# Sums joined in PSUM, a modulation pass issued earlier, and four triangular solves divided between two engines

## The chip, the core and the metric

The kernel runs on one core of a Trainium2 chip. The core has a matrix engine (TensorE, PE in the profile, with its weight loads shown as PEld), a vector engine (VectorE, DVE), an activation engine (ScalarE, ACT) and a general engine (GpSimd, POOL). SyncE (SP) only issues transfers. Every engine works through its own instructions in a fixed order and waits on semaphores. SBUF is the on-chip memory; PSUM holds the sums of TensorE in eight banks of 128 partitions x 512 f32. The metric is device time in microseconds (us) of one execution. The kernel of before took 1477.43 us, the median of three executions (1477.26 to 1480.0).

## The reference

One layer: an RMS norm with a modulation computed from `c`, one input projection whose columns are split over three groups of heads, an output projection, and a feed-forward block with a squared ReLU. There are 1024 latent tokens and 256 context tokens, and the width is 1024.

```python
def _project(h, lp, rope):
    z = h @ lp['w_in']
    f, aq, ak, av, dqkv, dz, gates = jnp.split(z, SPLITS, axis=-1)
    ...

def _chunk_gdn(q, k, v, g, beta, s0):          # chunks of 64 tokens, 4 heads
    ...
    lmat = jnp.where(strict, jnp.einsum('nbhid,nbhjd->nbhij', kb, kc) * decay, 0.0)
    tmat = lax.linalg.triangular_solve(eye + lmat, jnp.broadcast_to(eye, lmat.shape),
                                       left_side=True, lower=True)
    u = jnp.einsum('nbhij,nbhjd->nbhid', tmat, vb)
    ...
    s_fin, o = lax.scan(step, s0, (qc, kc, u, w, gc, qk))
```

The kernel uses chunks of 32 rows (its CK). The scan runs over them in two directions (d = 0 and 1), and each direction needs the inverse of a unit triangular matrix for every chunk and head. There are 32 latent and 8 context chunks.

## The kernel before

**Numbers.** A matmul operand is split into two parts, hi (rounded to f32r) and lo (the remainder), and a product is three matmuls into one bank: `mm3`, lines 238 to 241 (hi·hi, hi·lo, lo·hi). Single matmuls are issued by `mm` at line 236, transposes by `tp` at line 244, nearly all ACTIVATE instructions by `act` at line 223. In the rows below a line of a helper therefore stands for many callers, and the tile's name tells them apart.

**Stages, in us of the profiled execution.** Up to about 38, the first two modulation vectors are computed. Up to about 125 runs the k and v phase: for pairs of token tiles, `norm_in`, `trans_mod` (transposes, modulation, split into hi and lo) and `proj_N(w_kv, ...)` with `kv_sink`, which stores each tile in DRAM (`kvd`, line 524) after POOL's line 517; the k projection of the scan group, its convolution and the gates belong to the same stretch. From 125 to 205, q is projected in two halves of eight tiles (`proj_N(w_q, ...)`, `q_sink`, `qk_rows`, lines 499 to 517). From 205 to 345 the scan group's v and q are projected and convolved (`conv_proj`, `conv_silu`), and z and the Fourier columns are projected (`dz_f`, which stores z at line 818). Attention follows with the scan beside it (345 to 725), then the output projection (to 831), the second half's h of the feed-forward block (`h2_second`, in 831 to about 905), and the feed-forward products to the end.

**Modulation vectors.** `mod_steps` (line 314) computes one of six vectors from `w_mod`. For each of eight row blocks it loads a slab of 128 x 1024 f32 (512 KB) with an SP transfer (line 321), multiplies it in four matmuls (line 323, shown as L236) that fill four 32-row strips of one bank, and yields. Vectors 0 and 1 are needed first. The late ones are 3, 4, 2 and 5: vector 3 is computed by `mod_pass` ahead of the q projection, and 4, 2 and 5 in the task `modulations` (line 749), over two slab buffers (`msl`).

**Tasks.** `tick()` (line 450) is called inside projections after a few matmuls. It advances the generators in `tasks`, each given as [generator, every so many ticks, so many steps]. From the second half of q on these are `systems` (1, 3), `system1` (1, 1) and `modulations` (2, 1). `systems` first lets 12 steps pass, then runs `grams`: five rounds of 32 small matmuls on TensorE (line 706), two DVE products (line 709) and two stores to DRAM each. It then solves triangular systems: `solve(d, lat, eng)` loads its rows from DRAM and makes 30 elimination steps of two dependent instructions, a product (line 729) into `tmps[d]` and a sum (line 730). DVE solves the two context systems (32 partitions) step by step in turn, then latent direction 0 (128 partitions); POOL solves latent direction 1 from the end of `grams` on. Midway in `dz_f` (n == 3) both generators are run to their end.

**Order.** Instructions go to a scheduler that simulates a timeline and fixes each engine's order at build time. From the second half of q on, TensorE's instructions stay in program order (`pinned`). In the k and v phase they do not.

**Feed-forward block.** It multiplies 2 x 2 blocks of matrices with seven products in place of eight. `h2_second` (line 1539) transposes and modulates the second half of h and forms the sums of blocks that the products need (t1 to t4). The first half's blocks exist only as hi and lo (`HB["11"]`, `HB["21"]`), so a block is subtracted in two instructions, hi and then lo (line 1540). `split` (line 1454) makes the hi and lo of a result, with ACT rounding and the named engine subtracting. Each instruction covers 128 x 512.

Of the kernel before, what the change touches and what calls it, by code (L numbers as in the profile page):

```python
# [194 lines left out]
def body(tc, t, out):  # L195
# [3 lines left out]
    with ctx:  # L199
# [114 lines left out]
        def mod_steps(q, slabs, bank, queue=Y):  # L314
            w = t["w_mod"]
            for k in range(KT):
# [7 lines left out]
                yield  # L324
# [47 lines left out]
        def trans_mod(xs, a, s, hi, lo, banks, c0=0):  # L372
            w = len(xs) * P
            for k in range(KT):
# [6 lines left out]
                (G if k % 2 else V).tensor_tensor(lo[:, k, c0 : c0 + w], hf, f32(hi[:, k, c0 : c0 + w]), op=ALU.subtract)  # L381

# [43 lines left out]
        for b in slab0[4:] + slab1 + xTb:  # L426
            b.free()
# [98 lines left out]
        trb.items = bk[2:5]  # L526
# [6 lines left out]
        for b in xb + slab0[0:4] + hfb + [junkb]:  # L533
            b.free()
# [10 lines left out]
        msl = [buf(D) for _ in range(2)]  # L545
        mslr = Ring([b() for b in msl])
# [148 lines left out]
        done = []  # L695

        def grams():
            for c in list(range(NCL, NCA, 8)) + list(range(0, NCL, 8)):
# [12 lines left out]
                yield  # L711
            done.append(1)
# [3 lines left out]
        def solve(d, lat, eng):  # L716
# [7 lines left out]
            G.memset(Z2.base[pr_, at_ : at_ + S : CK + 1], 1.0)  # L724
# [10 lines left out]
        def systems():  # L735
            for _ in range(3 * GRAM):
                yield
            yield from grams()
            pair = [solve(d, False, V) for d in range(2)]
            while sum(next(x, 1) is None for x in pair):  # L740
                yield
            yield from solve(0, True, V)

        def system1():
            while not done:
                yield
            yield from solve(1, True, G)

        def modulations():
            (v,) = mod_rows(bk[2], 1, rowtmp())  # L750
            V.tensor_tensor(kt2(s2()), v, kt2(col[:, r_b2 : r_b2 + 8]), op=ALU.add)
            yield
            yield from mod_steps(4, mslr, bk[2])
            act(rowtmp(), bk[2][:, 0:256])
            yield
            (v,) = mod_rows(bk[2], 1, rowtmp())
            V.tensor_tensor(kt2(a2()), v, kt2(col[:, r_b2 + 8 : r_b2 + 16]), op=ALU.add)
            V.scalar_tensor_tensor(a2(), a2(), 1.0, col[:, r_n2 : r_n2 + 8], op0=ALU.add, op1=ALU.mult)
            yield
            for q, z in ((2, 0), (5, 1)):  # L760
                yield from mod_steps(q, mslr, bk[2])
                act(mrowb[z](), bk[2][:, 0:256])
                yield
# [1020 lines left out]
```

## Time and profile before

| | |
|---|---|
| three executions, median (lowest to highest) | 1477.43 us (1477.26 to 1480.0) |
| profiled execution, its own time | 1475.22 us |
| profiled execution, span of its trace | 1473.1 us |
| busy in the span: PE, DVE, ACT, POOL | 1391.9, 1026.7, 704.6, 657.2 us |
| mean granted TensorE clock | 0.972 |

The profiled execution is 2.21 us under the median and 2.1 us longer than its span. A row of the view of groups reads: line, engine, operation, output tile <- input tiles, shape, count | busy time and mean duration | idle time of that engine just before these instructions, and what ended it. A row of a timeline begins with start and duration in us. The clock is given as a share of full speed.

### The profile page before, as it was taken

To read this page: it belongs to the slowest core of one execution; us is meant where nothing else is said; L and a number is where in the kernel's file an instruction comes from. 1 tells how busy PE (TensorE), PEld (TensorE's weight loads), DVE (VectorE), ACT (ScalarE), POOL (GpSimd) and SP (SyncE) were. 2 spreads that over 40 slices of the span, in tenths; PEclk is the share of its full clock that TensorE was granted. 3 is DMA by queue.
4 is the path that set the end of the run, shared out by engine and by line. 5 is a ranking of instruction groups with operands and counts; after the bars stand their busy time and mean duration, and the time that the engine had idled before them with its cause. 6 is when DMAs were issued, how large, how long until landed. Compare 5 with 4: busy or idle time off the path is not lost.

```text
span 1473.1 us, 28890 instructions
## 1 busy us (share of the span) xinstructions
PE 1391.9 (94%) x11438; PEld 1118.6 (76%) x11438; DVE 1026.7 (70%) x1747; ACT 704.6 (48%) x1239; POOL 657.2 (45%) x698
## 2 busy tenths in 40 slices
PE   5899888989999999989899789999999999999998
PEld 1787866766777777768799667888888888888886
DVE  0876688775878777786733898755556677676884
ACT  1743312223777777776512645554555443443331
POOL 2764653632446466465433866444343100020782
PEclk8799999989999999999999889999999999999999
DMA  9414374552001010042222214544445898776641
GB/s 327 176 58 141 95 186 122 148 109 79 9 9 25 5 36 10 10 148 72 87 82 105 92 49 143 164 152 156 158 157 185 296 395 271 249 236 210 200 158 57
DMA packets 137302, 197.65 MB, mean 134 GB/s; under 512 B 45021, under 2 KB 80463, under 8 KB 136911
## 3 DMA queue, kind: packets, MB, share of 16 engines
q1 hardware_dynamic: 136464, 195.12, 41.2%
q8 instruction: 89, 1.46, 0.4%
q10 hardware_dynamic: 703, 0.69, 0.2%
q14 instruction: 46, 0.38, 0.1%
HBM read 149.84 MB, written 45.94 MB: 133 GB/s over the span
## 4 chain that ended last, share of the span: by engine, by line
PE 46%; DVE 5%; POOL 2%; issue 1%; DMA 1%; ACT 0%; DVEq 0%; POOLq 0%; ACTq 0%; SPq 0%
PE bk L240 8%; PE bk L241 8%; PE bk L239 8%; PE ba L239 7%; PE ba L240 7%; PE ba L241 7%; DVE fbase L1540 1%; PE bk L236 1%; DVE z1c L1454 1%; DVE z1b L1321 0%; DVE rbase L984 0%; DMA fbase<-la 0%; POOL rbase L1454 0%; PE ba L236 0%; POOL z2c L1714 0%
## 5 line engine op out<-in xcount | busy, mean ns | idle before, releaser
L223 ACT ACTIVATE rbase<-fbase 128x512 fp32r<-128x512 f32 (+3 forms) x255 | 171.9, 686 | 87.6 <-PE bk L240 55.3
L223 ACT ACTIVATE fbase<-bk 128x512 f32<-128x512 f32 (+3 forms) x224 | 124.9, 561 | 150.8 <-PE bk L236 93.8
L236 PE MATMUL bk<-rbase 128*128 128x256 f32 (+1 forms) x960 | 164.5, 307 | 2.1 <-DVE rbase L984 1.1
L236 PEld LDWEIGHTS bk<-rbase 128*128 128x128 f32 (+1 forms) x960 | 127.0, 173 | 30.4 <-DVE rbase L984 1.9
L236 PE MATMUL ba<-rbase 128*65 128x512 f32 (+4 forms) x576 | 137.7, 341 | 6.3 <-DVE rbase L984 4.6
L223 ACT ACTIVATE z1c<-fbase 128x512 fp32r<-128x512 f32 (+1 forms) x120 | 76.7, 654 | 135.3 <-DMA fbase<-w_ff 49.1
L223 ACT ACTIVATE fbase<-fbase 128x512 f32<-128x512 f32 (+4 forms) x148 | 95.8, 660 | 94.5 <-POOL fbase L1606 27.2
L1487 POOL TENSOR_TENSOR fbase<-fbase 128x512 f32<-128x512 f32 x64 | 89.2, 1395 | 110.7 <-DVE z1c L1454 101.5
L1688 POOL TENSOR_TENSOR z2c<-z2c,fbase 128x512 f32<-128x512 f32 x16 | 31.8, 2010 | 203.6 <-ACT z2c L223 128.6
L960 DVE TENSOR_REDUCE fbase<-ba 128x1 f32<-128x512 f32 (+1 forms) x192 | 106.4, 594 | 19.6 <-PE ba L236 18.2
L223 ACT ACTIVATE rbase<-z1d 128x1024 fp32r<-128x1024 f32 x61 | 63.1, 1055 | 101.2 <-PE bk L240 87.3
L1454 DVE TENSOR_TENSOR z1c<-fbase,z1c 128x512 fp32r<-128x512 f32 x112 | 96.3, 866 | 19.2 <-ACT z1c L223 15.8
L1454 DVE TENSOR_TENSOR rbase<-z1d,rbase 128x1024 fp32r<-128x1024 f32 x61 | 85.5, 1416 | 31.8 <-ACT rbase L223 31.7
L984 POOL TENSOR_TENSOR rbase<-fbase,rbase 128x512 fp32r<-128x512 f32 x56 | 72.1, 1288 | 67.2 <-ACT rbase L223 63.1
L239 PE MATMUL bk<-rbase 128*128 128x512 f32 x256 | 99.6, 389 | 0.0
L240 PE MATMUL bk<-rbase 128*128 128x512 f32 x256 | 99.6, 389 | 0.0
L241 PE MATMUL bk<-rbase 128*128 128x512 f32 x256 | 99.6, 389 | 0.0
L984 DVE TENSOR_TENSOR rbase<-fbase,rbase 128x512 fp32r<-128x512 f32 x104 | 81.0, 779 | 24.6 <-ACT rbase L223 23.9
L1454 DVE TENSOR_TENSOR rbase<-fbase,rbase 128x1024 fp32r<-128x1024 f32 (+1 forms) x63 | 79.7, 1285 | 22.6 <-ACT rbase L223 22.5
L236 PEld LDWEIGHTS ba<-rbase 128*65 128x65 f32 (+1 forms) x576 | 75.7, 154 | 23.9 <-DVE rbase L984 5.7
L240 PE MATMUL ba<-rbase 128*128 128x512 f32 x192 | 74.7, 389 | 0.0
L241 PE MATMUL ba<-rbase 128*128 128x512 f32 x192 | 74.7, 389 | 0.0
(346 smaller groups left out, 3842.6 us busy)
## 6 DMA issues: line engine op xcount, KB each, us to landing
fbase<-w_ff SPq DMA_DIRECT2D x70, 512.0 KB
u<-fbase SPq DMA_DIRECT2D x112, 256.0 KB
z1d<-w_ff SPq DMA_DIRECT2D x34, 512.0 KB
z1d<-u SPq DMA_DIRECT2D x33, 512.0 KB
fbase<-w_mod SPq DMA_DIRECT2D x32, 512.0 KB
fbase<-u SPq DMA_DIRECT2D x23, 512.0 KB
z2a<-w_mod SPq DMA_DIRECT2D x16, 512.0 KB
fbase<-w_in SPq DMA_DIRECT2D x16, 512.0 KB
```

The source lines that it names most:

```text
L223: return SC.activation(o, i, f, **k)
L236: pe(T.matmul(o, l, r, start=start, stop=stop))
L239: pe(T.matmul(o, lh, rh, start=start, stop=False))
L240: pe(T.matmul(o, lh, rl, start=False, stop=False))
L241: pe(T.matmul(o, ll, rh, start=False, stop=stop))
L960: V.tensor_reduce(st4[:, z : z + 1], b, AX.X, ALU.max)
L984: (G if k2 in GP and not any(a <= n < b for a, b in NGP) else V).tensor_tensor(hl[:, :, 1], p, f32(hl[:, :, 0]), op=ALU.subtract)
L1454: eng.tensor_tensor(lo, i, f32(hi), op=ALU.subtract)
L1487: G.tensor_tensor(w[nm], w[a], w[b], op=op)
L1540: sub = lambda e, o, i, x: e.tensor_tensor(o, i, x, op=ALU.subtract)
L1688: G.tensor_tensor(c, c, G2[cs_.start // 512], op=ALU.mult)
```

## The change

It has three parts.

**Sums joined in PSUM.** In `h2_second`, where a block is subtracted as hi and then lo, TensorE now multiplies hi and lo by the identity (`idb`, one new copy) into one bank of `tr2`, the ring of the transposes, and DVE subtracts that bank in one instruction. The splits of t3 and all subtractions of POOL in this function go to DVE.

**All late modulation vectors in the k and v phase.** `modulations` now computes vectors 3, 4, 2 and 5 and runs as a task from the start of the k and v phase, over five slab buffers and two slabs to a visit (`many`). `trans_mod` ticks too. Bank `bk[2]` is kept for it, so the transposes use `bk[3]`, `bk[4]` and `bk[1]` and the projection's ring is four banks. What is left of the task is run out after the last k and v tile.

**Solves.** DVE solves direction 0, context and then latent; POOL solves direction 1, context and then latent. Both tasks make three steps at every second tick. The wait ahead of `grams` is 4 steps in place of 12, and each of its rounds yields twice. The latent systems get buffers of their own (`trib`). At n == 3 only the context solves are run to their end.

```diff
@@ mod_steps, trans_mod @@
-        def mod_steps(q, slabs, bank, queue=Y):
+        def mod_steps(q, slabs, bank, queue=Y, many=1):
...
-                yield
+                if k % many == many - 1:
+                    yield
...
                 (G if k % 2 else V).tensor_tensor(lo[:, k, c0 : c0 + w], hf, f32(hi[:, k, c0 : c0 + w]), op=ALU.subtract)
+                if k % 4 == 1:
+                    tick()
@@ the k and v phase @@
-        for b in slab0[4:] + slab1 + xTb:
+        for b in slab0[7:] + slab1 + xTb:
             b.free()
...
-        trb.items = bk[2:5]
+        def modulations():
+            ring = Ring([b() for b in slab0[4:7] + late])
+            for q in (3, 4):
+                yield from mod_steps(q, ring, bk[2], Y, 2)
+                act(rowtmp(), bk[2][:, 0:256])
+                yield
+                (v,) = mod_rows(bk[2], 1, rowtmp())
...
+                yield
+            for q, z in ((2, 0), (5, 1)):
+                yield from mod_steps(q, ring, bk[2], Y, 2)
+                act(mrowb[z](), bk[2][:, 0:256])
+                yield
+
+        late = [buf(D) for _ in range(2)]
+        trb.items = bk[3:5] + [bk[1]]
+        mmr.items = A3 + [bk[0]]
+        tasks += [[modulations(), 1, 1]]
         for p, xs in enumerate((xs1, xs2, xs3, xs4)):
...
         proj_N(w_kv, 272, (8, 9), kv_sink)
+        for gen, _, _ in tasks:
+            for _ in gen:
+                pass
+        tasks.clear()
+        mmr.items = A3 + [bk[0], bk[1]]
@@ grams and solves @@
                     Y.dma_start(lsc[d][:, c : c + 8], l_)
                 yield
+                yield
...
-            at_ = kqt.at + (2 * d + 1 if lat else 1) * S
-            U = Z2.base[pr_, at_ : at_ + S].rearrange("p (m i) -> p m i", i=CK)
+            flat = trib[d]()[pr_] if lat else KQT[pr_, 0, 1, :]
+            U = flat.rearrange("p (m i) -> p m i", i=CK)
...
         def systems():
-            for _ in range(3 * GRAM):
+            for _ in range(GRAM):
                 yield
             yield from grams()
-            pair = [solve(d, False, V) for d in range(2)]
-            while sum(next(x, 1) is None for x in pair):
-                yield
+            yield from solve(0, False, V)
+            solved.append(1)
             yield from solve(0, True, V)
 
         def system1():
             while not done:
                 yield
+            yield from solve(1, False, G)
+            solved.append(1)
             yield from solve(1, True, G)
...
-        mod_pass(3, mslr, bk[2])
-        act(rowtmp(), bk[2][:, 0:256])
...
-                tasks += [[systems(), 1, 3], [system1(), 1, 1], [modulations(), 2, 1]]
+                tasks += [[systems(), 2, 3], [system1(), 2, 3]]
...
-                for gen, _, _ in tasks[0:2]:
-                    for _ in gen:
-                        pass
+                while len(solved) < 2:
+                    next(tasks[0][0])
+                    next(tasks[1][0])
@@ h2_second @@
+            def joined(nm, k):
+                b = tr2.next()
+                for z in range(2):
+                    mm(b, idb(), HB[nm][k][z], z == 0, z == 1)
+                return b
+
             for k in range(4):
                 h2_T(k, t1[k])
-                sub(G if k > 0 else V, t1[k], t1[k], f32(HB["11"][k][0]))
-                sub(V, t1[k], t1[k], f32(HB["11"][k][1]))
+                sub(t1[k], t1[k], joined("11", k))
                 split(t1[k], *HB["t1"][k], V)
...
             for k in range(4):
                 x3 = tr_.next()
-                sub(G, x3, t1[k], f32(HB["11"][k][0]))
-                sub(V, x3, x3, f32(HB["11"][k][1]))
-                split(x3, *HB["t3"][k], G)
-                sub(G, t1[k], t1[k], f32(HB["21"][k][0]))
-                sub(V, t1[k], t1[k], f32(HB["21"][k][1]))
+                sub(x3, t1[k], joined("11", k))
+                split(x3, *HB["t3"][k], V)
+                sub(t1[k], t1[k], joined("21", k))
                 split(t1[k], *HB["t4"][k], V)
```

How the built orders differ is shown at three places; the line numbers of the changed kernel are up to 30 higher there (its L758 is L729 of before, L784 is L770, L527 is L524).

SP's queue of the kernel before, where `dz_f` begins. A `w_mod` row is one slab, `zdr` takes the projected z, `tsc` and `lsc` carry the triangular systems:

```order
L439 DMA fbase<-w_in 128x4x256 x2
L321 DMA fbase<-w_mod 128x1024
L733 DMA tsc_1283<-z2a 8x32x32 x4
L321 DMA fbase<-w_mod 128x1024
L723 DMA z2a<-lsc_1280 32x32x32
L881 DMA fbase<-tsc_1283 128x256
L321 DMA fbase<-w_mod 128x1024 x3
L818 DMA zdr<-fbase 128x512
L321 DMA fbase<-w_mod 128x1024
```

The slabs stand there no more. They stand in SP's queue of the changed kernel at the end of the k and v phase, between the stores of k and v (`kvd`) and the loads of `w_in`:

```order
L321 DMA fbase<-w_mod 128x1024 x2
L321 DMA z2a<-w_mod 128x1024
L527 DMA kvd<-z2a 128x256
L442 DMA fbase<-w_in 128x4x256
L321 DMA z2a<-w_mod 128x1024
L442 DMA fbase<-w_in 128x4x256
L321 DMA z2a<-w_mod 128x1024
L527 DMA kvd<-z2a 128x256
L321 DMA fbase<-w_mod 128x1024 x2
```

POOL's order in the changed kernel in the second half of q, where L509 to L515 belong to `qk_rows` of the q tiles, and L758 and L759 are the two instructions of a step of the context system of direction 1:

```order
L753 MEMSET z2a 32x32
L758 TENSOR_TENSOR fbase<-z2a 32x30
L759 TENSOR_TENSOR z2a<-z2a,fbase 32x30
L758 TENSOR_TENSOR fbase<-z2a 32x58
L759 TENSOR_TENSOR z2a<-z2a,fbase 32x2x29
L758 TENSOR_TENSOR fbase<-z2a 32x84
L759 TENSOR_TENSOR z2a<-z2a,fbase 32x3x28
L509 TENSOR_SCALAR z2a<-z2a 128x4
L758 TENSOR_TENSOR fbase<-z2a 32x108
L510 TENSOR_TENSOR z2a<-z2a,fbase 128x4
```

Before, POOL had no instruction on 32-partition systems; they stood on DVE, beside the other direction's.

TensorE's order in `h2_second`, before (L244 are transposes, the bk_80 matmuls a feed-forward product that reads the sums):

```order
L239 MATMUL bk_78<-rbase,z1c 128x512
L240 MATMUL bk_78<-rbase,z1c 128x512
L241 MATMUL bk_78<-rbase,z1c 128x512
L244 MATMUL bk_79<-fbase 128x128 x4
L244 MATMUL bk_76<-fbase 128x128 x4
L244 MATMUL bk_77<-fbase 128x128 x4
L244 MATMUL bk_79<-fbase 128x128 x4
L239 MATMUL bk_80<-z2b,z1c 128x512
```

And the same place in the changed kernel, with the joins as pairs of L236:

```order
L236 MATMUL bk_79<-rbase 128x512 x2
L244 MATMUL bk_76<-fbase 128x128 x4
L236 MATMUL bk_77<-rbase 128x512 x2
L244 MATMUL bk_79<-fbase 128x128 x4
L239 MATMUL bk_80<-z2b,z1c 128x512
L240 MATMUL bk_80<-z2b,z1c 128x512
L241 MATMUL bk_80<-z2b,z1c 128x512
L236 MATMUL bk_76<-rbase 128x512 x2
```

A join stands between the transposes, and the product bk_80 begins after two joins more.

More of the change, by code (lines that the diff above doesn't have):

```diff
@@ L875, in body @@
         tasks.clear()
-        for b in [zrb, yb, csb, rowtmp, thc] + msl + tmps + lst.items:
+        for b in [zrb, yb, csb, rowtmp, thc] + trib + tmps + lst.items:
             b.free()
@@ L1432, in body @@
         tr2 = Ring([bk[0], bk[1]])
+        idb = rbuf(P)
+        V.tensor_copy(idb(), C["ident"])
         def rms_ff(q):
```

33 lines of the change are left out of this document (11 added, 22 removed).

## The prediction

> **What bounds the kernel now.** The page comes first, with the busy shares and the chain of work that ended last.
>
> ```profile
> PE 1391.9 (94%) x11438; PEld 1118.6 (76%) x11438; DVE 1026.7 (70%) x1747; ACT 704.6 (48%) x1239; POOL 657.2 (45%) x698
> PE 46%; DVE 5%; POOL 2%; issue 1%; DMA 1%; ACT 0%; DVEq 0%; POOLq 0%; ACTq 0%; SPq 0%
> ```
>
> TensorE is the bound over the whole, so the time can fall only where it stands idle, runs at a low clock or does needless work. The second view cuts the span into the stages that the change touches. Its columns are the stretch, its length, the busy time (and count) of PE, PEld, DVE, ACT and POOL, the granted clock, the DMA share and GB/s.
>
> ```profile
> 38.00:125.00 87.00, 82.52 (x518) 72.80 (x519) 68.06 (x158) 47.18 (x106) 55.44 (x97) 0.92 0.29 101
> 125.00:170.00 45.00, 43.24 (x595) 36.67 (x594) 25.38 (x42) 18.86 (x33) 25.96 (x22) 1.00 0.40 129
> 170.00:205.00 35.00, 25.57 (x476) 21.34 (x475) 28.86 (x82) 5.91 (x15) 17.26 (x29) 0.80 0.75 190
> 205.00:230.00 25.00, 20.79 (x124) 15.62 (x122) 23.77 (x63) 4.14 (x8) 13.90 (x17) 0.93 0.42 127
> 230.00:310.00 80.00, 70.57 (x664) 51.04 (x657) 65.66 (x113) 21.42 (x31) 45.26 (x65) 0.94 0.51 137
> 310.00:345.00 35.00, 35.00 (x432) 26.74 (x431) 20.41 (x42) 11.99 (x23) 6.34 (x7) 1.00 0.53 126
> 831.00:855.00 24.00, 13.89 (x48) 9.13 (x47) 22.63 (x24) 17.79 (x31) 15.39 (x10) 0.64 0.21 67
> 855.00:905.00 50.00, 48.50 (x189) 35.94 (x188) 46.10 (x50) 24.00 (x41) 38.48 (x23) 0.93 0.21 66
> ```
>
> From 125 to 345 us PE is busy for 195.2 of 220 us, idle for 24.8. From 831 to 855 it is idle for 10.1 of 24. The first is the q and convolution stretch, the second is `h2_second`. The third view, TensorE's waits, says on whom:
>
> ```profile
> PE bk L236 <- DMA fbase<-w_mod: 15.9, 7, 6.7
> ...
> PE bk L240 <- DVE z2b L1454: 5.8, 2, 4.9
> ...
> PE bk L706 <- DVE z2a L709: 4.7, 2, 3.1
> ...
> PE bk L244 <- ACT fbase L223: 4.4, 5, 1.7
> PE bk L236 <- DVE fbase L757: 2.3, 1, 2.3
> PE ba L241 <- POOL z1a L443: 1.9, 1, 1.9
> ```
>
> Of the 24.8 us, 15.9 go to slabs of the late modulation vectors, 2.3 to the readout between two vectors, 4.7 to the Gram products and 1.9 to a weight split. That is all of it.
>
> **Part 1: the late slabs leave the q and convolution stretch.** The groups by shape, from 40 to 345 us, have one row for all 256 late matmuls:
>
> ```profile
> L236 PE MATMUL bk<-fbase 128*32 128x256 f32 x256 | 22.6, 413 | 18.2 <-DMA fbase<-w_mod 15.9 <-DVE fbase L757 2.3
> ```
>
> The 22.6 us of work go from one stretch to another and count nothing in the sum. The 18.2 us of idle are the gain. Why a slab comes late is seen in SP's timeline, and in TensorE's just behind it:
>
> ```profile
> 285.51 0.33 SPq L321 DMA_DIRECT2D fbase<-w_mod  x1
> 296.69 0.33 SPq L818 DMA_DIRECT2D zdr<-fbase  x1
> 297.11 0.38 SPq L321 DMA_DIRECT2D fbase<-w_mod  x1
> ```
> ```profile
> 302.30 1.08 PE L236 MATMUL bk<-fbase 128*32 128x256 f32 x8 [6.74 <-DMA fbase<-w_mod]
> ```
>
> A slab stood behind a store of z that SP could not issue before 296.69, left at 297.11 and was used at 302.30, 5.2 us later. With the slabs gone from there, no `w_mod` row stands between these stores. I take **-18.2**.
>
> The Gram products wait for a bank that DVE has not read yet (4.7 us). Before, `systems` made three steps at each tick, so up to three rounds of `grams` fell on one tick. Now it makes 1.5 steps a tick and each round takes two, so DVE has a tick and more per round. I take **-4.7**, with 0 as the other end.
>
> After a gap the clock is lower. By the stage rows, work lost to it is at most 25.57 x 0.20 + 20.79 x 0.07 + 70.57 x 0.06 = 10.8 us from 170 to 310. The gaps that go are nearly all of them, and I take **-9** (0 to -11). Part 1 together: -32.
>
> **Part 2: what the k and v phase pays.** It takes up 22.6 us of TensorE work that is moved and 16.8 MB of slabs; it moved 101 GB/s at a DMA share of 0.29 before, so there is room. Slab pairs stand in SP's queue among the stores of k and v, as its order shows, and SP waits at such stores, eight times before:
>
> ```profile
> SPq L524 <- POOL z2a L517: 22.8, 8, 7.5
> ```
>
> SP was held 2.9 us a time there on the mean, 7.5 at the longest. The ring of five slabs is 2.5 visits deep. The phase lasts 87 us and will last some 110 with the moved work, for 16 visits: 6.9 us a visit at an even pace, so a slab is asked for some 17 us before its use where the queue is free, against 5.2 of flight and 2.9 of holding. But visits are not even, since the scheduler may put several side by side. I expect two late pairs, each 2 us late (7.5 + 5.2, less a lead that has shrunk to 11), and half as much again in clock: **+6**. The lower end is 0; at the upper end all of the 22.8 us reach TensorE with the same surcharge, +34. I stay near the lower end because the lead is longer than the mean hold and the flight together. Work on TensorE that waits behind a late slab is the projection itself, for which in turn nothing but ACT's readout waits.
>
> **Part 3: the solves.** The groups of the two solve lines, from 184 to 322 us:
>
> ```profile
> L729 DVE TENSOR_TENSOR fbase<-z2a 32x150 f32<-32x150 f32 (+29 forms) x90 | 38.8, 431 | 9.7 <-POOL z2a L730 4.2 <-DMA z2a<-lsc 2.7 <-POOL fbase L549 0.5
> L730 DVE TENSOR_TENSOR z2a<-z2a,fbase 32x150 f32<-32x150 f32 (+29 forms) x90 | 37.9, 421 | 2.4
> L729 POOL TENSOR_TENSOR fbase<-z2a 128x30 f32<-128x30 f32 (+14 forms) x30 | 19.7, 658 | 22.2 <-DVE z2a L730 20.9
> L730 POOL TENSOR_TENSOR z2a<-z2a,fbase 128x30 f32<-128x30 f32 (+14 forms) x30 | 19.4, 645 | 2.2
> ```
>
> DVE makes 180 instructions in 76.7 us, POOL 60 in 39.1, and POOL's latent solve waited 20.9 us for DVE's context solve of direction 1, which uses the same `tmps[1]`. Now each makes 120. DVE loses 60 x 0.426 = 25.6 us. Whether it keeps that gain depends on what its other 120 cost when POOL solves beside it, and that is in the timelines of DVE and, below, POOL:
>
> ```profile
> 282.32 4.45 DVE L729 TENSOR_TENSOR fbase<-z2a 128x58 f32<-128x58 f32 x1
> ...
> 288.92 0.69 DVE L729 TENSOR_TENSOR fbase<-z2a 128x108 f32<-128x108 f32 x1
> ...
> 316.64 0.27 DVE L729 TENSOR_TENSOR fbase<-z2a 128x108 f32<-128x108 f32 x1
> ```
> ```profile
> 282.21 4.49 POOL L802 TENSOR_TENSOR z2a<-z2a,fbase 128x2560 f32<-128x2560 f32 x1
> ...
> 288.86 0.62 POOL L729 TENSOR_TENSOR fbase<-z2a 128x238 f32<-128x238 f32 x1
> ```
>
> The same DVE instruction takes 0.27 us alone, 0.69 beside a POOL step, and one that met a large POOL instruction was held 4.45 us until that ended. So the remaining 120 cost 51 us (at 0.426) to 83 (at 0.69).
>
> The stage needs, from 125 to 345: TensorE 195.2 - 22.6 - 9 = 164 us. DVE has 164.1 us of busy time in the five rows; less 25.6 it needs 138.5 at best and 170 at worst. POOL has 108.7 and gets 60 more of 0.3 to 0.65, so 127 to 148. DVE thus goes from three quarters of the stretch to 84 to 104 per cent of what TensorE needs. Its densest stages before, 170 to 310, had it busy for 118.3 of 140 us, 0.84. At that density, 138.5 us take 165 and cost nothing, and 170 take 202 and cost TensorE 38. If a quarter of the 120 steps (30) are slowed from 0.426 to 0.69, DVE needs 146 and takes 174. I take that, **+10**, nearer the lower end: context and latent steps are spread at half the rate of ticks, the context solves are only due at n == 3, the latent ones by the end of the stretch, and up to 345 there are 35 us with DVE at 20.41. Queued behind a slow step on DVE stand the q tiles' L508 to L517, on which SP's store waits but no bank of TensorE, since ACT has read that already.
>
> *A rule that speaks against the split.* The Trainium skill, "SBUF — State Buffer", section "Who interferes with whom", says that a DVE instruction with two SBUF inputs contends with a GpSimd instruction that reads SBUF, and that the second to issue is blocked until the first has finished. By that rule, the trace agrees at 282 us (4.45 beside 4.49), and handing a solve to POOL saves DVE little; the sum would then be that of the rival of contention, for which the Trainium skill's rule stands as the reason.
>
> **Part 4: the joins.** From 831 to 855 us, DVE's groups, then POOL's:
>
> ```profile
> L1540 DVE TENSOR_TENSOR fbase<-fbase,rbase 128x512 f32<-128x512 f32 x5 | 7.6, 1517 | 0.0
> ...
> L1591 DVE TENSOR_TENSOR fbase<-ba,fbase 128x512 f32<-128x512 f32 x1 | 0.7, 678 | 0.0
> ```
> ```profile
> L1540 POOL TENSOR_TENSOR fbase<-fbase,rbase 128x512 f32<-128x512 f32 x3 | 5.1, 1713 | 0.0
> ```
>
> DVE is busy for 22.63 of these 24 us, and TensorE's longest wait here is for its split (4.9 of 5.8). Four blocks were subtracted by eight instructions, three of them on POOL. Now four on DVE do, with an operand in PSUM, for which L1591 gives 0.68: 2.7 in place of some 6.1 (four at 1.52) on DVE, and no POOL step of 1.71 in the chain. So DVE's stretch is 3.4 us shorter, and I take 5 for it with POOL's steps gone from the chain, and 2 for the clock (0.64 here): -7. A join is two matmuls on TensorE, 24 for all twelve. The step between two matmuls is in TensorE's timeline,
>
> ```profile
> 293.07 0.40 PE L241 MATMUL ba<-rbase,z1a 128*128 128x512 f32 x1
> 293.31 0.39 PE L239 MATMUL ba<-rbase,z1a 128*128 128x512 f32 x1
> ```
>
> 0.24 us, so 5.8 us in all. The first eight fall into idle time, the other 16 cost 3.8 where TensorE is 97% busy (855 to 905), for they stand between products. DVE's group of subtractions from 855 to 905 us is
>
> ```profile
> L1540 DVE TENSOR_TENSOR fbase<-fbase,rbase 128x512 f32<-128x512 f32 x8 | 13.7, 1726 | 1.2 <-POOL fbase L1540 1.2
> ```
>
> It has 46.10 of 50 us filled there and takes four splits over from POOL (2.7 us at 0.68), but sheds more, since these eight become eight with a PSUM operand (5.4 us). Sum **-4**; the ends are +6 (no wait goes) and, with all idle (11.6) and all lost clock (13.89 x 0.36 + 48.50 x 0.07 = 8.4) regained, -14.
>
> **Sum.** -32 + 6 + 10 - 4 = -20. Against the profiled execution's 1475.2 that is 1455; it lies 2.2 under the median, so of runs like those shown I expect 1477.4 - 20 = **1457**.
>
> **Rivals.**
> *All is regained.* The slabs hide in the k and v phase and DVE keeps pace: -32 + 0 + 0 - 10 = -42, 1435. For it speaks DVE at 138.5 of 164; against it, that two engines then run near full without holding TensorE once.
> *Contention takes the gain.* Half of DVE's steps, all those of the context, meet a POOL step and take 0.69: DVE needs 138.5 + 60 x 0.264 = 154, at its density 184, +20: -32 + 6 + 20 - 4 = -10, 1467. For it speak the rows at 288 us, and that POOL's large instructions (4.49) now meet more DVE steps.
> *The gap only changes its name.* TensorE waits for DVE where it waited for slabs, as DVE's solves were running up to 321 us anyway: +31 in part 3 (its end is +38), 1478.
> *Slower: slabs stall the k and v phase.* Each of the eight pairs that stand behind a store of k and v is loaded too late. It costs the flight of 5.2 us and 2.6 for the half clock after it (the stage from 831 has 0.64): 8 x 7.8 = 62 in place of 6, net +36, 1513. The sign turns where the eight pairs cost 26 us together, 3.3 each. For it speaks that SP is held 7.5 us at the longest; against it, the ring's lead.
>
> **Chances.** The forecast (1447 to 1463) 0.48, all regained (up to 1447) 0.20, contention 0.15, no change 0.06, slower 0.11. The range of 1437 to 1474 leaves out most of the last two and the far half of the first rival. A measurement here tells about 0.2% (3 us) from no change. Faster 0.83, within 0.2% 0.06, slower 0.11.
>
> **What would show it.** The groups of the changed kernel should have no wait on `w_mod` after 150 us, and L706 should wait under 1 us. In the k and v phase the matmuls of 256 columns should have under 6 us of idle before them; over 20 would be the slower rival. From 125 to 345, DVE should be busy for some 150 us of about 180; a TensorE that waits there for DVE or POOL by more than 15 us means contention. DVE's solve steps should be 0.45 to 0.65 us on the mean. L1540's successors should take 0.68 each, with TensorE's wait for L1454 gone. I am wrong above all if the convolutions on DVE turn out to be late behind solve steps.

## The result, and the profile after

The changed kernel takes 1464.84 us, the median of four executions (1461.87 to 1465.56), beside 1478.38 for the kernel before (1477.26 to 1480.0): a ratio of 0.9904, with an interval of 0.9886 to 0.9921. That is 13.5 us less. The profiled execution took 1465.56 us, and its span is 1463.8.

The page of the changed kernel, busy time by engine and the chain that ended last:

```profile
PE 1385.7 (95%) x11462; PEld 1119.9 (77%) x11462; DVE 1003.7 (69%) x1691; ACT 704.8 (48%) x1239; POOL 673.4 (46%) x743
PE 48%; DVE 2%; POOL 2%; DMA 1%; issue 1%; ACT 0%; DVEq 0%; SPq 0%; POOLq 0%; ACTq 0%
```

TensorE bounds it as before, with a smaller share of DVE in the chain (2% in place of 5). The stages of the changed kernel follow, with the columns of before. The k and v phase now reaches to about 138 us, and attention begins 4 us earlier, so a row holds somewhat other work than before; `h2_second` begins 2 us earlier, and the last row is set off by these.

```profile
38.00:125.00 87.00, 82.02 (x652) 62.33 (x651) 60.62 (x155) 46.08 (x102) 47.95 (x94) 0.94 0.79 281
125.00:170.00 45.00, 45.00 (x557) 39.29 (x556) 23.73 (x38) 20.27 (x36) 22.60 (x21) 1.00 0.12 37
170.00:205.00 35.00, 33.38 (x566) 32.37 (x565) 25.75 (x68) 7.57 (x16) 25.08 (x31) 1.00 0.38 105
205.00:230.00 25.00, 15.13 (x65) 11.71 (x64) 23.08 (x50) 5.24 (x11) 20.85 (x30) 0.80 0.46 77
230.00:310.00 80.00, 64.47 (x551) 53.38 (x551) 76.29 (x112) 22.34 (x31) 68.33 (x92) 0.89 0.17 44
310.00:345.00 35.00, 35.00 (x475) 26.02 (x473) 17.95 (x29) 11.73 (x23) 23.40 (x32) 1.00 0.63 146
829.00:853.00 24.00, 18.46 (x83) 13.77 (x82) 22.33 (x30) 20.57 (x36) 10.49 (x7) 0.93 0.21 66
```

Up to 205 us TensorE is all but full, and the slabs' traffic (281 GB/s in place of 101) costs it next to nothing: from 38 to 125 us it idles for 5.0 us, before for 4.5. From 205 to 310 it idles for 25.4 us. In the two rows from 205 to 310 us DVE is busy for 99.4 of 105 us and POOL for 89.2, where before they had 89.4 and 59.2. From 125 to 345 TensorE's idle time is 27.0 us, where it was 24.8, so it did not fall. Its waits in that window have other names:

```profile
PE ba L239 <- ACT z1a L223: 7.1, 1, 7.1
PE bk L241 <- POOL z1a L446: 6.5, 1, 6.5
PE bk L627 <- DVE fbase L601: 5.7, 1, 5.7
PE bk L241 <- DVE z1a L446: 3.2, 1, 3.2
PE ba L241 <- POOL z1a L446: 2.8, 1, 2.8
PE bk L734 <- DVE z2a L737: 1.6, 2, 0.9
```

No slab is waited for. The five large waits are for the preparation of weights (`z1a`: ACT makes hi, L446 makes lo) and for one convolution (L601). The late slabs' own groups, from 40 to 345 us, show it from the other side, 0.3 us of idle time in place of 18.2:

```profile
L236 PE MATMUL bk<-z2a,fbase 128*32 128x256 f32 x160 | 12.3, 389 | 0.3 <-DMA z2a<-w_mod 0.3
L236 PE MATMUL bk<-fbase 128*32 128x256 f32 x96 | 7.2, 387 | 0.0
```

Where, then, does the gain come from? The two profiled executions differ by 9.3 us in their spans (1473.1 and 1463.8), not by the 13.5 of the medians, and only these 9.3 can be given a place. In the feed-forward block DVE reads TensorE's products at one line. Its first and last start, before and after, mark the ends of the same work:

```profile
L1591 DVE TENSOR_TENSOR fbase<-bk,fbase x9: 676/691/692, 844.4 to 1134.6; 128x512 f32<-128x512 f32 x9
```
```profile
L1609 DVE TENSOR_TENSOR fbase<-bk,fbase x9: 675/690/692, 842.1 to 1125.3; 128x512 f32<-128x512 f32 x9
```

That is 290.2 us and then 283.2: 7.0 us went there. The other landmark is the first row maximum of attention (a DVE reduction), in the kernel before at 342.7 us and in the changed one at 338.5:

```profile
L960 DVE TENSOR_REDUCE fbase<-ba x192: 359/680/694, 342.7 to 702.8; 128x1 f32<-128x512 f32 x128, 128x1 f32<-128x256 f32 x64
```
```profile
L972 DVE TENSOR_REDUCE fbase<-ba x192: 357/679/705, 338.5 to 700.7; 128x1 f32<-128x512 f32 x128, 128x1 f32<-128x256 f32 x64
```

So by the start of attention the changed kernel is 4 us ahead, 2 of which are gone at its end. These 4 us are no idle time won. TensorE's work up to that point, 2904 matmuls in both, is shown by the stage view (before, then after):

```profile
0.00:342.70 342.70, 295.08 (x2904) 228.99 (x2904) 234.45 (x509) 117.99 (x233) 171.10 (x259) 0.93 0.51 152
```
```profile
0.00:338.50 338.50, 288.06 (x2904) 227.04 (x2904) 225.77 (x450) 119.21 (x233) 213.71 (x319) 0.93 0.48 150
```

TensorE idled for 47.6 us before and for 50.4 after, and as many matmuls took 7.0 us less. Nor are 4 us much here: two more executions of the code of before up to that point, shown with the experiments, reach it at 339.6 and 345.7 us, with matmul times of 291.4 and 296.9.

Three kinds of wait are followed back in the timelines of the engines. ACT, then TensorE, at the first matmul of the scan group's v:

```profile
209.64 0.38 ACT L223 ACTIVATE z2a<-bk 128x256 f32<-128x256 f32 x1 [7.89 <-POOL z2a L515]
...
213.15 1.04 ACT L223 ACTIVATE z1a<-fbase 128x1024 fp32r<-128x1024 f32 x1
```
```profile
214.25 0.80 PE L239 MATMUL ba<-rbase,z1a 128*128 128x512 f32 x1 [7.05 <-ACT z1a L223]
```

ACT stood for 7.89 us before a q tile whose buffer POOL had not finished with, since POOL made seven solve instructions of the context system in between (3.4 us of the wait), beside its own work on the q tiles. Behind that tile in ACT's queue stood the rounding of v's weights, for which TensorE waited. POOL's timeline at the scan group's q weights, then TensorE's:

```profile
245.80 0.74 POOL L759 TENSOR_TENSOR z2a<-z2a,fbase 32x240 f32<-32x240 f32 x1
246.61 0.61 POOL L758 TENSOR_TENSOR fbase<-z2a 32x240 f32<-32x240 f32 x1
...
253.67 0.57 POOL L758 TENSOR_TENSOR fbase<-z2a 32x210 f32<-32x210 f32 x1
254.32 2.34 POOL L446 TENSOR_TENSOR z1a<-fbase,z1a 128x1024 fp32r<-128x1024 f32 x1
```
```profile
256.71 0.79 PE L241 MATMUL bk<-rbase,z1a 128*128 128x512 f32 x1 [6.54 <-POOL z1a L446]
```

ACT had rounded both halves by 245.4 (243.38 and 2.00 us of work). POOL then made twelve more solve instructions, 8.5 us, before the split that TensorE waited for. On DVE the same happens at 306.97 with the split of the Fourier weights.

### The profile page after: what moved, and what is told of

Read it like the earlier page. It is cut to its first block, busy times and chain, and to the rows that moved or that the text cites. A ratio compares the mean times of both kernels' runs of the same rounds, so it can differ in the third digit from the quotient of the medians.

```text
span 1463.8 us, 28936 instructions
## 1 busy us (share of the span) xinstructions
PE 1385.7 (95%) x11462; PEld 1119.9 (77%) x11462; DVE 1003.7 (69%) x1691; ACT 704.8 (48%) x1239; POOL 673.4 (46%) x743
## 4 chain that ended last, share of the span: by engine, by line
PE 48%; DVE 2%; POOL 2%; DMA 1%; issue 1%; ACT 0%; DVEq 0%; SPq 0%; POOLq 0%; ACTq 0%
PE bk L240 8%; PE bk L239 8%; PE bk L241 8%; PE ba L239 7%; PE ba L240 7%; PE ba L241 7%; PE bk L236 2%; DVE z1b L1333 0%; PE ba L236 0%; POOL rbase L1468 0%; DMA fbase<-x 0%; PE bk L244 0%; DVE rbase L996 0%; POOL z2c L1734 0%; POOL z2c L1732 0%
## 5 line engine op out<-in xcount | busy, mean ns | idle before, releaser
L236 PE MATMUL bk<-rbase 128*128 128x256 f32 (+2 forms) x984 | 173.1, 311 | 4.6 <-ACT fbase L223 2.5
L236 PEld LDWEIGHTS bk<-rbase 128*128 128x128 f32 (+1 forms) x984 | 132.2, 175 | 34.2 <-ACT fbase L223 3.3
L236 PE MATMUL ba<-rbase 128*65 128x512 f32 (+4 forms) x576 | 138.4, 342 | 6.2 <-DVE rbase L996 4.8
L1468 DVE TENSOR_TENSOR z1c<-fbase,z1c 128x512 fp32r<-128x512 f32 x112 | 91.2, 818 | 24.0 <-ACT z1c L223 20.8
L236 PEld LDWEIGHTS ba<-rbase 128*65 128x65 f32 (+1 forms) x576 | 76.1, 155 | 24.1 <-DVE rbase L996 5.9
```

Of the source, the lines that this page charges most:

```text
L236: pe(T.matmul(o, l, r, start=start, stop=stop))
L1468: eng.tensor_tensor(lo, i, f32(hi), op=ALU.subtract)
```

## The experiments

Each kernel was timed in three rounds against the kernel before on the same chip. Its ratio to that kernel is given with the interval.

**The parts added one by one.** First the joins alone, in the kernel before:

```diff
-                sub(V, t1[k], t1[k], f32(HB["11"][k][0]))
+                sub(t1[k], t1[k], joined("11", k))
...
```

> The kernel before with the joins alone. Theory 1 (each part is worth what the stretch it touches gained): about -7 against before, since between the ninth feed-forward product and its like the changed kernel gained 7.0 us (the product read at 844.4 there, 842.1 after, the one at 1134.6 there, 1125.3 after). Theory 2 (the joins gain only because the work before them arrives earlier or with POOL idle): under 3.

1466.55 us, 0.9922 (0.9902 to 0.9942). The marked feed-forward stretch takes 283.0 us (840.6 to 1123.6), so 7.2 of the gain are the joins by place. That stretch hardly scatters: it takes 282.9 to 283.2 us in the profiles of all twelve kernels here that have the joins, and 290.2 and 289.8 in the two that have not. Of the rest of the 11 us, 3.1 lie ahead of attention, where this kernel has the instructions of before in the same order. How much that part scatters is seen from the first row maximum in three executions of it: 342.7 us before, 339.6 here, 345.7 in a run below. One profile a kernel can therefore not settle a few microseconds ahead of attention, and the joins are worth some 7 us by place.

Then the early slabs on top of the joins, with the solves as they were:

```diff
-                tasks += [[systems(), 2, 3], [system1(), 2, 3]]
+                tasks += [[systems(), 1, 3], [system1(), 1, 1]]
...
-                while len(solved) < 2:
-                    next(tasks[0][0])
-                    next(tasks[1][0])
+                for gen, _, _ in tasks[0:2]:
+                    for _ in gen:
+                        pass
```

> The changed kernel with grams and solves as before (DVE three systems, POOL one, ticks 1, 3 and 1, 1, all run out at n == 3). Theory 1 (with the slabs gone, the solve steps that stand ahead of weight splits and convolutions are what TensorE waits for, and giving POOL a second system is what brought them in front of POOL's splits): the 9.3 us of idle before POOL's splits go, but DVE's longer chain ends later, so 1462 to 1470, within 5 us of the changed kernel. Theory 2 (splitting the solves is a loss by the shared port): 1450 to 1458. Theory 3 (DVE's chain of three systems is the bound once the slabs are gone): over 1472.

1484.15 us, 1.0043 (1.0028 to 1.0058): slower than before, though the joins are in it, as theory 3 had it. TensorE's waits begin with

```profile
PE bk L613 <- ACT fbase L223: 20.9, 1, 20.9
```

one wait of 20.9 us, in the q norm that follows the point n == 3, where all solves are run to their end. The slabs' waits are gone, TensorE arrives sooner, and DVE's chain of three systems is as long as ever.

Next, on top of that, buffers for the latent systems, so that only the context is due at n == 3. DVE still has both context systems, and POOL begins its latent system when they are done:

```diff
+        trib = [buf(S) for _ in range(2)]
...
+            flat = trib[d]()[pr_] if lat else KQT[pr_, 0, 1, :]
...
+                while len(solved) < 2:
+                    next(tasks[0][0])
+                    next(tasks[1][0])
```

> The run with the old solves and early slabs (1484), with one part of the change added: buffers of their own for the latent systems, so that only the context is run to its end at n == 3. DVE still solves both context systems, ticks as before. Theory A (that run lost its time in the 20.9 us in which TensorE waited at n == 3 for the latent solves): 1458 to 1466. Theory B (the early slabs make the q phase denser and that costs, whatever the solves): 1470 or more.

1466.22 us, 0.9928 (0.9907 to 0.995), 0.2 past the edge of what theory A had. The 20.9 us are gone, and two waits on DVE stand in their place, 12.8 us for the convolution L601 and 5.5 for a split. So deferring the latent solves takes back the 18 us that the early slabs had cost with the old solves, with no division of work.

Then the slower ticks and the earlier, spread Gram rounds as in the changed kernel, DVE still with both context systems. The edit is shown against the changed kernel:

```diff
-            yield from solve(0, False, V)
+            pair = [solve(d, False, V) for d in range(2)]
+            while sum(next(x, 1) is None for x in pair):
+                yield
             solved.append(1)
...
-            while not done:
+            while not solved:
                 yield
-            yield from solve(1, False, G)
             solved.append(1)
             yield from solve(1, True, G)
```

> The changed kernel with both context systems on DVE, step by step in turn as before, and POOL with latent direction 1 alone, from the end of the context on; ticks, buffers and the run at n == 3 as in the changed kernel. Theory A: POOL's splits and the q tiles are free of solve steps, the gaps of 7.1, 2.8 and 6.5 us go, while DVE gets 60 steps of 0.25 to 0.42 us more, 20 us, in a stretch where it is full: 1458 to 1468. Theory B (steps cost more because two engines run them at once): context steps take 0.3 us alone and the whole is faster, 1450 to 1458.

1460.27 us, 0.9879 (0.9848 to 0.991). Its one step to the changed kernel (1464.84, 0.9886 to 0.9921) gives POOL the second context system. The intervals overlap, so a loss of 4.5 us isn't shown, but a gain from dividing the context isn't either. It lies in theory A's range and over theory B's. By place, the wait for POOL's split of the scan-q weights is gone, ACT's and POOL's on the v weights are 4.6 and 2.2, and the wait for L601 has grown to 11.8. The gap moved from POOL's queue to DVE's.

**The price of the steps.** The changed kernel without the solves' arithmetic, so that no triangular system is solved:

```diff
-                eng.tensor_tensor(tv, ...)
-                eng.tensor_tensor(U[:, ms, is_], ...)
+                if False:
+                    eng.tensor_tensor(tv, ...)
+                    eng.tensor_tensor(U[:, ms, is_], ...)
```

> The changed kernel without the 240 product and sum instructions of the solves, so that the triangular systems are not solved; their loads, stores and ticks stay. Theory 1 (solve steps cause the gaps of the convolutions): of the 25.4 us of idle between 207 and 310 at least 20 go and the clock with them, 1435 to 1445. Theory 2 (the gaps come from weight loads that stand behind stores on SP, or from the q tiles' chain): 1455 or more, gaps at the same places.

1438.15 us, 0.9732 (0.9714 to 0.975), so 26.7 us under the changed kernel. Its stage from 230 to 310:

```profile
230.00:310.00 80.00, 80.00 (x888) 65.29 (x887) 34.59 (x37) 30.93 (x49) 13.75 (x16) 1.00 0.26 72
```

TensorE is full at full clock here. The first row maximum comes at 310.8 instead of 338.5. That is theory 1, with one exception: a gap of 4.9 us before POOL's split for v is there with no solve step at all, and no other is over 1 us. So at the v weights, where the changed kernel waits for 7.1 and 2.8 us, a wait of 5.6 us (0.7 and 4.9) is not the steps' doing. The two runs after this one have `if eng is G` and `if eng is V` in that place: the first leaves out DVE's steps (direction 0), the second POOL's (direction 1).

> The changed kernel without DVE's 120 solve steps (direction 0 is not solved), POOL's 120 stay. Without any step it took 1438, with all 1465. Theory A (order: each engine's steps delay what stands behind them there): POOL's gaps (7.1, 2.8 and 6.5 us) stay, DVE's (5.7 and 3.2) go, 1450 to 1456; POOL's steps stay near 0.67 us. Theory B (the two engines slow each other): POOL's steps fall under 0.5 us and all gaps shrink, 1440 to 1447.

1443.86 us, 0.9775 (0.9744 to 0.9806).

> The changed kernel without POOL's 120 solve steps (direction 1 is not solved), DVE's 120 stay. Theory A: POOL's gaps (7.1, 2.8 and 6.5 us) go, DVE's (5.7 and 3.2) stay, 1446 to 1452. Theory B: DVE's steps fall from 0.53 to 0.40 us or less and all gaps shrink, 1438 to 1444.

1444.94 us, 0.9776 (0.9746 to 0.9806). Either half of the steps alone costs 6 or 7 us over none, and both together 27: the times are theory B's, in the second 0.9 past its edge. But the steps' own durations do not follow it on POOL. The groups of POOL's context system (the first two rows are the changed kernel's, from 184 to 340 us, the last two those of the run with POOL alone, from 170 to 345):

```profile
L758 POOL TENSOR_TENSOR fbase<-z2a 32x30 f32<-32x30 f32 (+14 forms) x30 | 22.2, 740 | 2.3
L759 POOL TENSOR_TENSOR z2a<-z2a,fbase 32x30 f32<-32x30 f32 (+14 forms) x30 | 20.2, 674 | 2.4
```
```profile
L759 POOL TENSOR_TENSOR fbase<-z2a 32x30 f32<-32x30 f32 (+14 forms) x30 | 18.4, 612 | 2.4
L760 POOL TENSOR_TENSOR z2a<-z2a,fbase 32x30 f32<-32x30 f32 (+14 forms) x30 | 20.1, 668 | 2.4
```

and one group each of DVE's latent and context systems, with DVE alone in the last two rows (the changed kernel's rows first):

```profile
L758 DVE TENSOR_TENSOR fbase<-fbase 128x30 f32<-128x30 f32 (+14 forms) x30 | 18.1, 602 | 0.8
L758 DVE TENSOR_TENSOR fbase<-z2a 32x30 f32<-32x30 f32 (+14 forms) x30 | 16.2, 539 | 1.6 <-DMA z2a<-lsc 1.2
```
```profile
L759 DVE TENSOR_TENSOR fbase<-fbase 128x30 f32<-128x30 f32 (+14 forms) x30 | 9.9, 330 | 0.8
L759 DVE TENSOR_TENSOR fbase<-z2a 32x30 f32<-32x30 f32 (+14 forms) x30 | 9.5, 315 | 1.0 <-DMA z2a<-lsc 0.5
```

Over all four groups of an engine, DVE's 120 steps take 63.9 us beside POOL and 47.3 alone, POOL's 80.9 and 77.2. So DVE pays 16.6 us for the company and POOL 3.7. Nor did the gaps stay with their engine, as theory A had it: without POOL's steps the wait of 6.5 us before its split of the scan-q weights went, but so did DVE's of 3.2, while the one before the v split rose from 2.8 to 5.6; and without DVE's steps the 6.5 shrank to 1.3. Nor is a full POOL enough to hold TensorE: with POOL's steps alone it was busy for 73.0 of the 80 us from 230 on, more than the 68.3 in the changed kernel, and made three solve instructions between the rounding of the scan-q weights and its split, in place of twelve. What the runs show is the joint condition. With one engine's steps gone, the other's cost 6 or 7 us; with both, DVE and POOL fill the stretch and the steps cost 27.

**Moving what waits.** Slower ticks put weight splits ahead of more solve steps:

```diff
-                tasks += [[systems(), 2, 3], [system1(), 2, 3]]
+                tasks += [[systems(), 3, 2], [system1(), 3, 2]]
```

> The changed kernel with both solve tasks at two steps on every third tick (0.67 a tick in place of 1.5), which puts POOL's second split of the v weights after 3 solve steps in place of 7 and the splits of the q weights after 17 in place of 20. Theory 1 (splits wait behind solve steps): the first two gaps of the convolutions (7.1 and 2.8 us) shrink by 4 to 8, the run at n == 3 grows by some of it, so 1457 to 1465. Theory 2 (both engines are full, whatever the order): within 3 us of the changed kernel, with the gaps elsewhere.

1462.85 us, 0.9899 (0.9875 to 0.9924). The first gap shrank from 7.1 to 2.9 us, but the others became 4.1, 6.7, 7.0 and 2.6: 23.3 in all in place of 25.4. It is within 2 us of the changed kernel, which theory 2 had and theory 1's range holds as well; the gaps moved.

```diff
-        w_dv = wgroup([(COL_DV, 256)], G)
+        w_dv = wgroup([(COL_DV, 256)])
...
-        w_dq = wgroup([(COL_DQ, 256)], G)
+        w_dq = wgroup([(COL_DQ, 256)])
```

> The changed kernel with the splits of the v and scan-q weights on DVE in place of POOL. Theory 1 (a split waits behind the solve steps of its engine, POOL's more than DVE's): the gaps of 2.8 and 6.5 us before POOL's splits go and 1 to 4 us come on DVE, 1456 to 1462. Theory 2 (DVE is the fuller engine, busy for 76.3 of 80 us from 230 to 310): four splits of 1.25 us more on it make later gaps longer, 1463 to 1470.

1460.72 us, 0.9886 (0.986 to 0.9911). The time falls in theory 1's range, but not as it was told: the gaps before these splits are still there, on DVE now, 3.1 and 4.4 us where POOL had 2.8 and 6.5, and what shrank is ACT's wait (1.7 in place of 7.1), while the waits for the convolution L601 grew from 5.7 to 7.9. The time lies 4 us under the changed kernel's, with intervals that overlap.

```diff
-        wfz = [wgroup([(COL_DZ, 256)])]
+        wfz = [wgroup([(COL_DZ, 256)], G)]
...
-                wfz.append(wgroup([(COL_F, 256)]))
+                wfz.append(wgroup([(COL_F, 256)], G))
```

> The run with both context systems on DVE (1460.3), and the splits of the z and Fourier weights on POOL too. There DVE was busy for 75.4 of 80 us from 230 to 310 and TensorE waited 11.8 us for a convolution and 2.8 for a split on DVE, while POOL was busy for 38.5. Theory A (DVE is what TensorE waits for in that stretch): 5 us less on DVE, 3 to 7 us faster, 1453 to 1457. Theory B (POOL's instructions of 2.5 us hold DVE's up by as much as they relieve it): within 3 us of 1460.

This one is built on the run with both context systems on DVE. 1467.16 us, 0.9932 (0.9914 to 0.995): worse than that run by 7, which neither theory had. The wait for L601 grew from 11.8 to 13.6, and one for the q norm, L614, of 2.4 came up. DVE gave away four splits, 5.7 us at 1.43 each, but its 180 solve steps took 86.7 us where they had taken 80.1, and its busy time up to attention went from 231.9 to 233.2. That is the mechanism of theory B, at a price that it did not foresee: taking splits from the fuller engine did not relieve it.

The next is built on that one and moves work in TensorE's order:

```diff
-        compact(dst, 1, VC, 0.5)
...
+            if n == 2:
+                compact(dst, 1, VC, 0.5)
...
+            if n == 5:
+                conv_proj(w_dq, 0, (0, 1))
```

> As the run before it in this list, and in TensorE's order the transposes of the second v half, which waited 11.8 us for their convolution on DVE, stand three steps of the z projection later, the last scan-q projection and the end of the context solves two steps later. Theory A (DVE's convolution is late by a fixed amount, and other matmuls can fill the gap): 3 to 8 us faster than that run. Theory B (the z weights' own splits are late too, and the gap moves to them): within 3 us of it.

1467.61 us, 0.9944 (0.9925 to 0.9963), theory B. In this kernel the last scan-q projection reads the Fourier weights, which by then have taken the buffers of its own, so part of the computation is another. The wait for L601 fell to 4.1 us, and 4.1 on POOL's split and 7.0 on a load of k and v, both new, took its place.

**What the joins are made of.** The kernel before, with POOL taken out of `h2_second` and no joins:

```diff
-                sub(G if k > 0 else V, t1[k], t1[k], f32(HB["11"][k][0]))
+                sub(V, t1[k], t1[k], f32(HB["11"][k][0]))
...
-                sub(G, x3, t1[k], f32(HB["11"][k][0]))
+                sub(V, x3, t1[k], f32(HB["11"][k][0]))
...
-                split(x3, *HB["t3"][k], G)
-                sub(G, t1[k], t1[k], f32(HB["21"][k][0]))
+                split(x3, *HB["t3"][k], V)
+                sub(V, t1[k], t1[k], f32(HB["21"][k][0]))
```

> The kernel before with all subtractions and splits of the second half's sums on DVE, POOL out of it, and no joins: 24 subtractions and the four splits of t3 stay separate instructions. The joins alone took 7.0 us out of the feed-forward stretch (290.2 to 283.0 us between the first and the last read of a product from a bk bank). Theory 1 (the gain comes from POOL no longer slowing DVE): the 24 subtractions take about 0.69 us each, 16.6 us, and the stretch gains 4 to 7. Theory 2 (it comes from halving the instructions, with an operand in PSUM): the stretch gains at most 2, since DVE has 12 instructions more than with joins, 8 us.

1473.41 us, 0.9984 (0.9968 to 1.0). The marked stretch:

```profile
L1591 DVE TENSOR_TENSOR fbase<-bk,fbase x9: 677/690/692, 850.4 to 1140.2; 128x512 f32<-128x512 f32 x9
```

289.8 us against 290.2, so the gain is 0.4: theory 2. The 24 subtractions fell to a median of 0.68 us, as theory 1 said, but there are 12 more of them than with joins, and that eats the relief. So taking POOL out is not enough by itself. Joins with POOL still subtracting were not run, so whether the halved number of instructions would do alone stays open.

## Why the prediction held in sum and not in its terms

The forecast was 1457 (-20) and the range 1437 to 1474; it came to -13.5, inside the range and 2 us above the narrower forecast of 1447 to 1463. The sum was -32 + 6 + 10 - 4. Term by term:

**Part 1, the waits that go (-18.2 and -4.7): right.** The slabs' 18.2 us became 0.3, and the Gram wait 1.6, where I had asked for under 1. The clock (-9) failed. By the stage rows, at most 15.13 x 0.20 + 64.47 x 0.11 = 10.1 us are lost to it from 205 to 310, against 10.8 before from 170 to 310. The clock follows the gaps (1.00 in the rows without them, 0.80 and 0.89 from 205 to 310), and new gaps came.

**Part 2, the k and v phase (+6): mis-sized, 0.** No slab was late by more than 0.3 us there. The ring's lead held even where visits stand side by side. The rival in which this phase makes the kernel slower fell with it.

**Part 3, the solves (+10): the step that failed in size.** The gaps are 25.4 us, where only the 1.9 of a split had been there besides the waits of part 1, and without the steps 26.7 us go. DVE's work was nearly as I had it: a quarter of its 120 steps slowed makes 59 us, and they took 63.9. I had given POOL's context steps 0.3 to 0.65 us, and they took 0.71 (42.4 us for 60). (The stage rows from 125 to 345 have 166.8 us for DVE and 160.3 for POOL, where I had at most 170 and 148, but that window now reaches 13 us into the k and v phase; up to the first row maximum DVE is busy for 225.8 us where it was 234.5.) What failed is the step from busy time to waits. I charged TensorE for DVE's work by the density of the stretch before, and TensorE waited for single instructions behind others in three queues. And one sentence of it was wrong in kind. It named what stands behind a slow step on DVE, q tiles, and found that no bank of TensorE waits for them. It did not ask the same of ACT's queue, where the rounding of weights stands behind those q tiles, nor of POOL's, where the splits stand behind the steps. Those two queues hold 16.4 of the 25.4 us, of which 5.6 are there without steps too. The place I named as the thing to go wrong, convolutions behind solve steps, is the 5.7 of L601.

**Part 4, the joins (-4): right in kind, mis-sized, -7.0.** DVE's twelve subtractions take 0.68 us each, no POOL instruction is left among them, and TensorE's wait for L1454 of 5.8 us is gone. I had charged 3.8 us for the matmuls from 855 on. They displaced waits instead: from 829 to 853 TensorE is busy for 18.46 of 24 us at a clock of 0.93, where it had 13.89 at 0.64. The clock was the larger part, and I had given it 2 us: by the stage rows at most 8.4 us were lost to it from 831 to 905 before, and 18.46 x 0.07 = 1.3 after, since the next 50 us now run at 1.00 in place of 0.93.

In place of -16 for the slabs and solves and -4 for the joins stand some -2 to -6.5 and -7 to -11, as the joins alone gave 0.9922 and all of it 0.9904, with intervals that overlap; so it is not shown that slabs and solves gain anything on top of the joins. That the time fell inside the range is partly luck: the waits of part 1, the clock and part 3 came out some 2, 8 and 13.5 us dearer than I had them, the k and v phase and the joins 6 and 3 cheaper. With these the terms come to some -5, where the profiles differ by 9.3. In between lie the 7.0 us less of matmul time ahead of attention and the 2 us lost during attention, and what made them is not shown. The rival that came nearest is the gap that changes its name, which I gave 0.06, for part 3; its time (1478) missed because the k and v phase cost nothing and the joins gave more. Contention, at 1467, lies 2 us from the time, and by the sign that I had set for it (TensorE waits for DVE or POOL by more than 15 us from 125 to 345) the profile speaks for it: those waits come to 19.8 us. The rule of the Trainium skill ("SBUF — State Buffer", "Who interferes with whom") pointed that way and holds for what DVE lost (16.6 us over its 120 steps). A lock that blocks either one would let the GpSimd side lose too, and here it lost 3.7; why is not shown.

What stays open is how much of the 27 us is order and how much is fullness. Every move of a split or a step in a kernel that does the whole work moved the gaps, and none removed them. No version that does the whole work beats the changed kernel beyond its interval; the fastest two (1460.27 and 1460.72) lie 4 us under it.

## What to carry to other kernels

Before moving an idle wait out of a stretch, add up the other engines' work there against what the bound engine will then need: here DVE went to 95% and POOL to 85% of the 80 us from 230 on, and the 18 us that the slabs gave back came in again as waits for weight preparation. Go through the queue of every engine that takes on work, and ask of each instruction behind it who waits; a helper engine's queue can hold a split that TensorE needs. And take a part of a bundle on its own before crediting it: of this one, the joins alone carried 11 of the 13.5 us by the medians, early slabs with the old solves made the kernel slower, and what paid in the solves was a buffer that let half of them be late.

## What the runs showed of the hardware

A POOL step on 32 partitions (0.74 and 0.67 us) took no less than one on 128 (0.63 and 0.65), while the lengths per partition were the same, so fewer partitions saved nothing. And two engines on two-input work in SBUF do not share the cost: over 120 steps each, DVE's mean rose from 0.394 to 0.532 us and POOL's from 0.643 to 0.674. A DVE step beside a large POOL instruction is held for nearly all of it, in the changed kernel 2.54 us where the step before took 0.39:

```profile
215.63 2.61 POOL L446 TENSOR_TENSOR z1a<-fbase,z1a 128x1024 fp32r<-128x1024 f32 x1
```
```profile
214.74 0.39 DVE L758 TENSOR_TENSOR fbase<-z2a 32x234 f32<-32x234 f32 x1
...
215.96 2.54 DVE L758 TENSOR_TENSOR fbase<-z2a 32x238 f32<-32x238 f32 x1
```

And a DVE subtraction on 128x512 f32 takes its short time with one operand in PSUM as well as without POOL beside it: in the changed kernel twelve with an operand in PSUM took 0.67 to 0.69 us, in the run without joins and without POOL the median of 24 with both operands in SBUF is 0.68, and before, with POOL subtracting beside them, the median of 13 was 1.77.
